# Second feed-forward product of a decoder layer: where GpSimd's sums, their loads and the side work stand in the order, and the first loads of a seam

## The chip, the cores and the metric

One core of a Trainium2 chip runs the whole program in one launch. The metric is the time of an execution on the device, in microseconds (us). Before the change three executions took 2927.35, 2926.52 and 2920.95 us; the median is 2926.52.

The engines have these names in the profile: PE is TensorE (matrix products), ACT is ScalarE, DVE is VectorE, POOL is GpSimd, and SP is SyncE, which here only issues DMA transfers (SPq in the profile). Each engine works through its own instructions in the order of the program and waits at an instruction until the data and the buffer that it needs are there.

## The reference

One layer of a decoder: a feed-forward network (FFN), token mixing by two branches (a pooling branch and a state-space branch), and a second FFN, on 1024 prompt tokens and 64 sample tokens, in float32. Cut to what matters here:

```python
def swiglu(x, w_in, w_out):
    gu = x @ w_in
    g, u = gu[..., :D_FF], gu[..., D_FF:]
    return (jax.nn.silu(g) * u) @ w_out

def layer(x, pool_hist, out_pos0, conv_hist, h0, l):
    x = x + 0.5 * swiglu(rmsnorm(x, norm_ffn1[l]), ffn1_w_in[l], ffn1_w_out[l])
    mix, ... = token_mixing(rmsnorm(x, norm_mix[l]), ...)
    x = x + mix
    x = x + 0.5 * swiglu(rmsnorm(x, norm_ffn2[l]), ffn2_w_in[l], ffn2_w_out[l])
    return x, ...

# in token_mixing: d is the trailing-window mean minus the token, in four groups of channels
y = jnp.einsum('btgc,gcd->btgd', d, w_group).reshape(Bsz, T, POOL_WIDTH)
```

D_MODEL is 1024, D_FF is 2816. The change touches the products with `w_out` of both FFNs, and the loads of `d` for the product with `w_group`.

## The kernel before

**Numbers.** Each float32 operand is split in a high part and a rest (`hh` and `hr` or the two halves of `hp` for the hidden values, `wh` and `wl` for weights): ACT writes the high part (L769, L787), DVE the rest (L770, L788), and PE adds three products, high x high, rest x high and high x low. The 1088 tokens are held in two halves of 512 and 576 tokens; a "pair" of matmuls below is the same step for both halves.

**The second product.** `second()` computes hidden x `w_out` in seven products of half the size (Strassen's scheme in a form with shared sums), in the order "1256473". A product has four units m (128 output channels each), and a unit has 11 blocks of k, whose weights come in three chunks of 4, 4 and 3 blocks. So a unit is 11 x 3 matmuls for each half, 66 in all. Product "3" is done half by half at the end; the others do both halves in a unit.

- The left operands (X) are sums of hidden blocks that the first product left in DRAM (`hb`). `fetch_X` loads them (L762, tiles `hr` and `hp`) and `split_X` splits them. `AHEAD` says how many of the next product's blocks are fetched behind a unit.
- The right operands are weights or sums of weights. `raw` loads a chunk (L776); for "1", "2" and "4" that is all. For "5" POOL adds two loaded chunks (L805, tile `ws`, kept), for "6" it subtracts a third from the kept one (L809), for "7" it takes a new difference (L814). `fourth(m)`, called behind each unit of "4", turns the kept chunk into the weights of "3" (L821, with one load at L776 into a `ws` tile).
- `leave` takes a unit's result out of PSUM on DVE (L863). After a unit of "6" it reloads a part of x from DRAM (L882, tile `x`), to which POOL adds after "4" (L885). `old` loads parts of the residual x after units of "6" and "7" (L827, tile `xo`); the additions on POOL (L833) are put into the list `late_` and made when the next unit is at its last chunk.

**Side work.** While FFN1 runs, `part` splits weights of later products and stores both parts in DRAM (load L313, tile `pr`; ACT L317, tile `ph`; DVE L318; stores L320 and L321). It is a generator that `tick` steps whenever PE's planned time has reached its due time; `finish(side)` runs what is left of it at once. FFN2 has no side work.

**The seam.** The pooling branch reads `d` (high part `dh`, rest `dl`) from DRAM, for two halves h and eight blocks k, two blocks for each of the four groups of channels (L1416). Six blocks are loaded ahead, at the end of the projections, the others by `fetch_d` one group ahead.

**What sets the order.** Python's order is only a start. A scheduler orders the instructions of each engine by its own estimate of times and by priorities (`tc.high_priority`), within the dependences; `pin` (that is, `tc.keep_in_program_order`) keeps an instruction in source order among those of its engine that are pinned too. Before the change pinned are, in this part, ACT's splits of X (L769), the side work's (L317) and POOL's sums L805 and L809, but not L814, L821, L833 and L885, nor the loads.

The buffers that bound how far a load can run ahead: six tiles for raw weights (`wraw`), three each for `wh` and `wl`, four `ws` tiles for the loads of "7" and of `fourth`.

Of the kernel before, what the change touches and what calls it, by code (L numbers as in the profile page):

```python
# [65 lines left out]
def tile_hybrid_pool_ssd_macaron(  # L66
# [588 lines left out]
    def ffn(wi, wo, prep, after, half, side=None):  # L655

        def plain(x):
            for ff in range(N_PLAIN[x[0]]):  # L660
                ffn_in_plain(wi, ff, x)

        X = operands(prep, plain)
        if side:
            side = start(side, PART_AT)
        for ff in range(N_PLAIN[1], N_PLAIN[0]):
            ffn_in(wi, ff, [(1, X[1])])
        for ff in range(N_PLAIN[0], NFF - N_APART):
            ffn_in(wi, ff, [(h, X[h]) for h in HALVES])
        front, run = second(wo, after, half)  # L670
        for h in HALVES:
            for ff in range(NFF - N_APART, NFF):
                if (h, ff) == (0, NFF - 1):
                    f = start(front(), X_FRONT)
                ffn_in(wi, ff, [(h, X[h])])
        if side:
            finish(side)
        finish(f)
        run()
# [62 lines left out]
    def second(wo, after, half):  # L742
# [29 lines left out]
        def raw(par, mh, m, kb, nk, t=None):  # L772
            if t is None:
                t = sp.tile([P, 4 * P], F32, tag="wraw", bufs=N_RAW, name=nm("wraw"))[:, : nk * P]
            c0 = (mh * 4 + m) * P
            dma(t.rearrange("p (k c) -> p k c", c=P), wv[par][:, kb : kb + nk, c0 : c0 + P])  # L776
            return t
# [13 lines left out]
        def weights(p, m):  # L791
            for kb, nk in chunks:
# [17 lines left out]
                else:  # L810
                    a = stage["p"].tile([P, 4 * P], F32, tag="wsum", bufs=N_S, name=nm("ws"))[:, : nk * P]
                    x, y = raw(0, 0, m, kb, nk, a), raw(0, 1, m, kb, nk)
                    with tc.high_priority(hp[0]):
                        G.tensor_tensor(a, x, y, op=ALU.subtract)  # L814
                yield (kb, nk) + parts(a, nk, ring("wh", nk), ring("wl", nk))

        def fourth(m):
            for kb, nk in chunks:
                t = stage["p"].tile([P, 4 * P], F32, tag="wsum", bufs=N_S, name=nm("ws"))[:, : nk * P]
                a, x = held[m, kb], raw(1, 0, m, kb, nk, t)  # L820
                G.tensor_tensor(a, x, a, op=ALU.subtract)  # L821

        def old(m, q, col):
            t = act((P, 576), name="xo")
            for h in HALVES:
                n, at = NPAIR[h], HALF_AT[h]
                dma(t[:, at : at + n], xspill[h][4 * q + m][:, col * n : (col + 1) * n])  # L827

            def put():
                for h in HALVES:  # L830
                    n, at = NPAIR[h], HALF_AT[h]
                    o = xt[h][4 * q + m][:, col * n : (col + 1) * n]
                    G.tensor_tensor(o, o, t[:, at : at + n], op=ALU.add)  # L833
# [24 lines left out]
        def leave(p, m, h, pt):  # L858
# [24 lines left out]
            elif p == "4":  # L883
                add(b[:, f], b[:, f])
                G.tensor_tensor(b[:, s_], b[:, s_], a[:, s_], op=ALU.add)  # L885
# [13 lines left out]
        def run():  # L899
            fetch_X("1", NK2)  # L900
            split_X(4)
            for p, nxt in zip(order[:-1], order[1:]):
# [3 lines left out]
                for m in range(4):  # L906
# [6 lines left out]
                    if p == "4":  # L913
                        fourth(m)
                    while p == "1" and hlast:
# [452 lines left out]
    def in_proj(prep):  # L1368
# [32 lines left out]
        ahead_d = []  # L1401
        for k in range(6):
            ahead_d.append(load_d(0, k))
# [57 lines left out]
    def pool_branch():  # L1461

        f = [([None] * KD, [None] * KD) for h in HALVES]
        d = dict(enumerate(ahead_d)), {}
# [553 lines left out]
```

## Time and profile before

| | us |
|---|---|
| executions (median 2926.52) | 2927.35, 2926.52, 2920.95 |
| profiled execution | 2930.37 |
| its span on the core | 2928.4 |
| mean granted clock of PE | 0.98 |
| second product of FFN1 | 529.11 to 794.06 |
| second product of FFN2 | 2656.97 to 2912.00 |
| seam into the pooling branch | about 1515 to 1560 |

The prediction quotes the views. A row of a timeline has the start and the duration in us, the engine, the line, the operation, its output and inputs, and how many instructions were merged; in brackets stands the idle time just before and what ended it. A row of the windows has the stretch, its length, the busy time of PE, PE's weight loads, DVE, ACT and POOL, the granted clock, the share of the DMA engines and GB/s. A row of the waits has who waited for whom: us in total, how often, the longest. Starts lie on one axis, from the span's start.

### The profile page before, as it was taken

Reading aid. Unit: us, or ns where it says so; the run is one execution under the profiler, and the core shown is the slowest. Engines: PE = TensorE matmul, PEld = TensorE weight load, DVE = VectorE, ACT = ScalarE, POOL = GpSimd, SP = SyncE. Lnnn points to the kernel's source line nnn. Section 1 sums busy time; section 2 is a strip of 40 time slices with the busy share of each in tenths; the row PEclk is TensorE's granted clock in tenths of the full one; section 3 lists DMA queues with packets and bytes.
Section 4 is the critical chain, followed back from the end, with each engine's and each line's share of the span. In section 5 each row is a group of like instructions: output and inputs, shape, how many; then the busy total and the mean of one; then the engine's idle time right before and its main releaser. Section 6 shows DMA issues by size and latency. Waiting matters only on the chain. (4 is left out here: it accounts for less than half of the span.)

```text
span 2928.4 us, 54549 instructions
## 1 busy us (share of the span) xinstructions
PE 2796.4 (95%) x19834; PEld 2617.3 (89%) x19834; DVE 1848.0 (63%) x2848; ACT 1399.7 (48%) x3086; POOL 1365.1 (47%) x1424
## 2 busy tenths in 40 slices
PE   7999999998999999999989999898999999999988
PEld 6999999898889999999988887677999999999987
DVE  6656556675784586866766767766666454556855
ACT  5444444433444555554546567576234444444333
POOL 5466566154542355554622333323225666561642
PEclk9999999999999999999999999998999999999999
DMA  4466545777445455543376567785674342336773
GB/s 123 146 195 213 160 151 173 222 220 236 149 124 166 149 181 173 188 132 122 106 238 201 184 232 231 246 254 185 228 252 145 112 125 88 99 122 208 225 226 107
DMA packets 567437, 515.25 MB, mean 176 GB/s; under 512 B 37876, under 2 KB 436072, under 8 KB 567160
## 3 DMA queue, kind: packets, MB, share of 16 engines
q1 hardware_dynamic: 564848, 507.31, 55.1%
q10 hardware_dynamic: 2320, 4.46, 0.4%
q8 instruction: 156, 2.56, 0.4%
q14 instruction: 113, 0.93, 0.1%
HBM read 363.51 MB, written 148.36 MB: 175 GB/s over the span
## 5 line engine op out<-in xcount | busy, mean ns | idle before, releaser
L167 PE MATMUL pw<-X,wh 128*128 128x288 f32 (+2 forms) x2832 | 627.2, 310 | 4.5 <-ACT v L569 4.5
L167 PEld LDWEIGHTS pw<-X,wh 128*128 128x128 f32 x2832 | 462.2, 189 | 26.9 <-ACT v L569 5.4
L167 PE MATMUL pw<-X,wl 128*128 128x288 f32 (+1 forms) x1644 | 473.9, 288 | 0.0
L167 PE MATMUL pw<-hl,wh 128*128 128x256 f32 (+1 forms) x1536 | 394.4, 329 | 0.6 <-ACT wh L452 0.4
L453 DVE TENSOR_TENSOR wl<-s,wh 128x512 fp32r<-128x512 f32 x288 | 231.7, 806 | 255.0 <-ACT wh L452 241.7
L446 POOL TENSOR_TENSOR s<-wraw,wraw 128x512 f32<-128x512 f32 x144 | 199.3, 1384 | 338.5 <-DVE wl L453 211.0
L167 PE MATMUL pw<-hi,wh 128*128 128x288 f32 x1120 | 330.8, 295 | 0.0
L167 PE MATMUL pw<-hi,wl 128*128 128x288 f32 x1120 | 329.8, 294 | 0.0
L167 PE MATMUL pw<-lo,wh 128*128 128x288 f32 x1120 | 329.7, 294 | 0.0
L167 PEld LDWEIGHTS pw<-X,wl 128*128 128x128 f32 x1644 | 312.0, 190 | 0.1
L167 PE MATMUL pw<-hl,wl 128*128 128x256 f32 x1072 | 301.4, 281 | 1.2 <-DVE wl L453 1.2
L167 PEld LDWEIGHTS pw<-hl,wh 128*128 128x128 f32 x1536 | 260.0, 190 | 22.1 <-ACT wh L452 0.6
L452 ACT ACTIVATE wh<-s 128x512 fp32r<-128x512 f32 x288 | 180.9, 630 | 163.4 <-PE pw L167 140.1
L453 DVE TENSOR_TENSOR wl<-wraw,wh 128x512 fp32r<-128x512 f32 x216 | 172.6, 799 | 135.2 <-ACT wh L452 126.7
L452 ACT ACTIVATE wh<-wraw 128x512 fp32r<-128x512 f32 x216 | 135.6, 628 | 174.1 <-PE pw L167 151.4
L167 PEld LDWEIGHTS pw<-hi,wh 128*128 128x128 f32 x1120 | 210.7, 188 | 6.4
L167 PEld LDWEIGHTS pw<-lo,wh 128*128 128x128 f32 x1120 | 210.7, 188 | 0.0
L167 PEld LDWEIGHTS pw<-hi,wl 128*128 128x128 f32 x1120 | 210.2, 188 | 0.0
L167 PEld LDWEIGHTS pw<-hl,wl 128*128 128x128 f32 x1072 | 204.1, 190 | 1.4 <-DVE wl L453 1.4
L167 PE MATMUL po<-hh,wh 128*128 128x256 f32 (+1 forms) x848 | 185.9, 290 | 5.8 <-ACT hh L769 5.8
L167 PE MATMUL po<-hr,wh 128*128 128x256 f32 (+1 forms) x848 | 186.9, 291 | 3.2 <-DVE hr L770 3.2
L167 PE MATMUL pso<-yhl,wh 128*128 128x288 f32 (+1 forms) x768 | 181.8, 339 | 4.8 <-ACT acc L1818 3.3
(400 smaller groups left out, 6844.9 us busy)
## 6 DMA issues: line engine op xcount, KB each, us to landing
wraw<-in_ffn_w_in_dram SPq DMA_DIRECT2D x188, 256.0 KB
wraw<-in_w_in_dram SPq DMA_DIRECT2D x144, 256.0 KB
wh<-part SPq DMA_DIRECT2D x116, 256.0 KB
wl<-part SPq DMA_DIRECT2D x116, 256.0 KB
hr<-hb SPq DMA_DIRECT2D x106, 272.0 KB
wraw<-in_ffn_w_out_dram SPq DMA_DIRECT2D x96, 256.0 KB
hb<-g SPq DMA_DIRECT2D x66, 288.0 KB
hb<-g SPq DMA_DIRECT2D x66, 256.0 KB
```

The costliest lines, as they stand in the source:

```text
L167: T.matmul(out, lhsT, rhs, start=start, stop=stop, skip_group_check=free)
L446: G.tensor_tensor(t, a, b, op=op)
L452: S.activation(wh, a, AF.Copy)
L453: V.tensor_tensor(wl, a, wh.bitcast(F32), op=ALU.subtract)
```

## The change

Three parts:

1. `ffn` no longer finishes the side work before the second product. It hands `side` to `run`, which finishes it behind the first unit of product "2".
2. In `second`, the loads of `fourth` are pinned, and so are POOL's differences for "7" (L814) and "3" (L821), the additions of the old x (L833) with their loads (L827), and the addition in `leave` after "4" (L885).
3. Of the six blocks of `d` that are loaded ahead, two are now of the second half: (0,0), (0,1), (1,0), (1,1), (0,2), (0,3) in place of the first half's 0 to 5.

```diff
@@ -673,10 +673,8 @@
                 if (h, ff) == (0, NFF - 1):
                     f = start(front(), X_FRONT)
                 ffn_in(wi, ff, [(h, X[h])])
-        if side:
-            finish(side)
         finish(f)
-        run()
+        run(side)
 
     def rest(c, gen):
         finish(c)
@@ -769,11 +767,13 @@
                 pin(S.activation(a, r, AF.Copy))
                 V.tensor_tensor(r.bitcast(F32R), r, a.bitcast(F32), op=ALU.subtract)
 
-        def raw(par, mh, m, kb, nk, t=None):
+        def raw(par, mh, m, kb, nk, t=None, fixed=False):
             if t is None:
                 t = sp.tile([P, 4 * P], F32, tag="wraw", bufs=N_RAW, name=nm("wraw"))[:, : nk * P]
             c0 = (mh * 4 + m) * P
-            dma(t.rearrange("p (k c) -> p k c", c=P), wv[par][:, kb : kb + nk, c0 : c0 + P])
+            ld = dma(t.rearrange("p (k c) -> p k c", c=P), wv[par][:, kb : kb + nk, c0 : c0 + P])
+            if fixed:
+                pin(ld)
             return t
 
         def ring(tag, nk):
@@ -811,26 +811,26 @@
                     a = stage["p"].tile([P, 4 * P], F32, tag="wsum", bufs=N_S, name=nm("ws"))[:, : nk * P]
                     x, y = raw(0, 0, m, kb, nk, a), raw(0, 1, m, kb, nk)
                     with tc.high_priority(hp[0]):
-                        G.tensor_tensor(a, x, y, op=ALU.subtract)
+                        pin(G.tensor_tensor(a, x, y, op=ALU.subtract))
                 yield (kb, nk) + parts(a, nk, ring("wh", nk), ring("wl", nk))
 
         def fourth(m):
             for kb, nk in chunks:
                 t = stage["p"].tile([P, 4 * P], F32, tag="wsum", bufs=N_S, name=nm("ws"))[:, : nk * P]
-                a, x = held[m, kb], raw(1, 0, m, kb, nk, t)
-                G.tensor_tensor(a, x, a, op=ALU.subtract)
+                a, x = held[m, kb], raw(1, 0, m, kb, nk, t, True)
+                pin(G.tensor_tensor(a, x, a, op=ALU.subtract))
 
         def old(m, q, col):
             t = act((P, 576), name="xo")
             for h in HALVES:
                 n, at = NPAIR[h], HALF_AT[h]
-                dma(t[:, at : at + n], xspill[h][4 * q + m][:, col * n : (col + 1) * n])
+                pin(dma(t[:, at : at + n], xspill[h][4 * q + m][:, col * n : (col + 1) * n]))
 
             def put():
                 for h in HALVES:
                     n, at = NPAIR[h], HALF_AT[h]
                     o = xt[h][4 * q + m][:, col * n : (col + 1) * n]
-                    G.tensor_tensor(o, o, t[:, at : at + n], op=ALU.add)
+                    pin(G.tensor_tensor(o, o, t[:, at : at + n], op=ALU.add))
 
             late_.append(put)
 
@@ -882,7 +882,7 @@
                 dma(b[:, s_], xspill[h][4 + m][:, s_])
             elif p == "4":
                 add(b[:, f], b[:, f])
-                G.tensor_tensor(b[:, s_], b[:, s_], a[:, s_], op=ALU.add)
+                pin(G.tensor_tensor(b[:, s_], b[:, s_], a[:, s_], op=ALU.add))
             elif p == "7":
                 add(b[:, f], b[:, f])
                 add(b[:, s_], b[:, s_])
@@ -896,7 +896,7 @@
                 split_X(k + 1)
                 yield 1.0
 
-        def run():
+        def run(side):
             fetch_X("1", NK2)
             split_X(4)
             for p, nxt in zip(order[:-1], order[1:]):
@@ -912,6 +912,8 @@
                         old(m, 0, 1)
                     if p == "4":
                         fourth(m)
+                    if side and p == "2" and m == 0:
+                        finish(side)
                     while p == "1" and hlast:
                         hlast.pop(0)()
                     while p == "1" and m == 2 and hsums:
@@ -1398,9 +1400,9 @@
             for kind, ia, ib in (("c", 16 + g, 20 + g), ("c", 4 * g, 4 * g + 1), ("c", 4 * g + 2, 4 * g + 3),
                                  ("u", 2 * g, 2 * g + 1), ("z", 4 * g, 4 * g + 1), ("z", 4 * g + 2, 4 * g + 3)):
                 proj_pair(kind, ia, ib, both)
-        ahead_d = []
-        for k in range(6):
-            ahead_d.append(load_d(0, k))
+        ahead_d = [{}, {}]
+        for h, k in ((0, 0), (0, 1), (1, 0), (1, 1), (0, 2), (0, 3)):
+            ahead_d[h][k] = load_d(h, k)
         for i in range(N_GATE[1], N_GATE[0], 2):
             proj_pair("g", i, i + 1, both[1:])
         last[0] = True
@@ -1461,7 +1463,7 @@
     def pool_branch():
 
         f = [([None] * KD, [None] * KD) for h in HALVES]
-        d = dict(enumerate(ahead_d)), {}
+        d = ahead_d
 
         def fetch_d(gi):
             for h in HALVES:
```

What this does to the order, at three places. In the names a number tells tiles apart; the lines are those of each kernel, so L762, L769 and L776 of before are L760, L767 and L774 in the changed one.

**ACT at the start of FFN1's second product.** `wh<-wraw` are weights of unit 0 of "1", `hh<-hr` blocks of X, `ph<-pr` side work, `g` is the end of the first product. Before:

```order
L787 ACTIVATE wh_6352<-wraw_6350 128x512
L787 ACTIVATE wh_6382<-wraw_6380 128x512
L610 ACTIVATE g_6166<-g_6166 128x288
L769 ACTIVATE hh_6168<-hr_6169 128x544
L769 ACTIVATE hh_6171<-hr_6172 128x544
L317 ACTIVATE ph_6310<-pr_6208 128x512
L787 ACTIVATE wh_6414<-wraw_6412 128x384
L317 ACTIVATE ph_6319<-pr_6317 128x512
L769 ACTIVATE hh_6174<-hr_6175 128x544
L769 ACTIVATE hh_6177<-hr_6178 128x544
L769 ACTIVATE hh_6180<-hr_6181 128x544
```

After the change:

```order
L787 ACTIVATE wh_6336<-wraw_6334 128x512
L317 ACTIVATE ph_6358<-pr_6208 128x512
L787 ACTIVATE wh_6373<-wraw_6371 128x512
L767 ACTIVATE hh_6320<-hr_6321 128x544
L610 ACTIVATE g_6166<-g_6166 128x288
L767 ACTIVATE hh_6168<-hr_6169 128x544
L767 ACTIVATE hh_6171<-hr_6172 128x544
L767 ACTIVATE hh_6174<-hr_6175 128x544
L767 ACTIVATE hh_6177<-hr_6178 128x544
L767 ACTIVATE hh_6180<-hr_6181 128x544
L767 ACTIVATE hh_6183<-hr_6184 128x544
```

The second of the two side splits, of `pr_6317`, is gone from here (the changed kernel has it as `pr_6403`, behind the second unit's X); one more block of X, `hr_6321`, stands early, and the third chunk of weights behind the blocks of X.

**SP from product "6" into "4" of FFN1** (FFN2 has the same). `xo` are the old x, `x<-xspill` the reload of `leave`, `ws` loads for the fourth sums, `wraw_8080` and up weights of "4", `hr` blocks of X for "4". Before:

```order
L827 DMA xo_7730<-xspill_0_83 128x256
L827 DMA xo_7730<-xspill_0_91 128x288
L827 DMA xo_7842<-xspill_1_84 128x256
L827 DMA xo_7842<-xspill_1_92 128x288
L762 DMA hr_7848<-hb_4_285 128x544
L762 DMA hr_7851<-hb_5_289 128x544
L776 DMA wraw_8080<-in_ffn_w_out_dram 128x4x128
L776 DMA wraw_8110<-in_ffn_w_out_dram 128x4x128
L776 DMA wraw_8140<-in_ffn_w_out_dram 128x3x128
L776 DMA wraw_8193<-in_ffn_w_out_dram 128x4x128
L776 DMA wraw_8223<-in_ffn_w_out_dram 128x4x128
L882 DMA x_7283<-xspill_4_87 128x256
```

After the change:

```order
L882 DMA x_7283<-xspill_4_87 128x256
L882 DMA x_7285<-xspill_4_95 128x288
L827 DMA xo_7730<-xspill_0_83 128x256
L827 DMA xo_7730<-xspill_0_91 128x288
L774 DMA wraw_8080<-in_ffn_w_out_dram 128x4x128
L774 DMA wraw_8110<-in_ffn_w_out_dram 128x4x128
L774 DMA wraw_8140<-in_ffn_w_out_dram 128x3x128
L774 DMA ws_8176<-in_ffn_w_out_dram 128x4x128
L774 DMA ws_8179<-in_ffn_w_out_dram 128x4x128
L882 DMA x_7394<-xspill_5_88 128x256
L774 DMA ws_8182<-in_ffn_w_out_dram 128x3x128
L882 DMA x_7396<-xspill_5_96 128x288
```

The reload of unit 0 (`x_7283`, `x_7285`) now precedes the old x of its unit, and the old x of unit 1 (`xo_7842`) goes behind the weights, the first fourth loads and the reload of unit 1. Before, eight more `ws` loads stood in one block behind `x_7285`; now they stand apart, the later ones behind the last X of "4".

**POOL in product "7" of FFN1** (FFN2 likewise). L814 of `ws_8769`, `ws_8802` and `ws_8835` are the weights of the third unit, of `ws_8890` and up those of the fourth. Before:

```order
L833 TENSOR_TENSOR x_6863<-x_6863,xo_8635 128x256
L833 TENSOR_TENSOR x_6865<-x_6865,xo_8635 128x288
L833 TENSOR_TENSOR x_6965<-x_6965,xo_8756 128x256
L833 TENSOR_TENSOR x_6967<-x_6967,xo_8756 128x288
L833 TENSOR_TENSOR x_7283<-x_7283,xo_8632 128x256
L814 TENSOR_TENSOR ws_8769<-ws_8769,wraw_8771 128x512
L833 TENSOR_TENSOR x_7285<-x_7285,xo_8632 128x288
L814 TENSOR_TENSOR ws_8802<-ws_8802,wraw_8804 128x512
L814 TENSOR_TENSOR ws_8835<-ws_8835,wraw_8837 128x384
L814 TENSOR_TENSOR ws_8890<-ws_8890,wraw_8892 128x512
L814 TENSOR_TENSOR ws_8923<-ws_8923,wraw_8925 128x512
```

After the change:

```order
L833 TENSOR_TENSOR x_7283<-x_7283,xo_8632 128x256
L833 TENSOR_TENSOR x_7285<-x_7285,xo_8632 128x288
L833 TENSOR_TENSOR x_6863<-x_6863,xo_8635 128x256
L833 TENSOR_TENSOR x_6865<-x_6865,xo_8635 128x288
L814 TENSOR_TENSOR ws_8769<-ws_8769,wraw_8771 128x512
L814 TENSOR_TENSOR ws_8802<-ws_8802,wraw_8804 128x512
L814 TENSOR_TENSOR ws_8835<-ws_8835,wraw_8837 128x384
L833 TENSOR_TENSOR x_7394<-x_7394,xo_8753 128x256
L833 TENSOR_TENSOR x_7396<-x_7396,xo_8753 128x288
L833 TENSOR_TENSOR x_6965<-x_6965,xo_8756 128x256
L833 TENSOR_TENSOR x_6967<-x_6967,xo_8756 128x288
L814 TENSOR_TENSOR ws_8890<-ws_8890,wraw_8892 128x512
```

The additions (L833) of a unit now stand together and ahead of the sums of the unit after the next: four instead of five before `ws_8769`, and four more before `ws_8890`.

## The prediction, made before the changed kernel was run

> **What bounds the kernel now.** I read the busy shares first, then the two stretches that hold the second product of each feed-forward network (FFN), then PE's waits. TensorE (PE) sets the end: it is busy 95% of the span, so a change pays only where PE stands still or runs slow.
>
> ```profile
> PE 2796.4 (95%) x19834; PEld 2617.3 (89%) x19834; DVE 1848.0 (63%) x2848; ACT 1399.7 (48%) x3086; POOL 1365.1 (47%) x1424
> ...
> 529.11:794.06 264.95, 243.80 (x1865) 240.82 (x1865) 177.71 (x250) 105.36 (x189) 113.96 (x97) 0.95 0.71 212
> 2656.97:2912.00 255.03, 238.84 (x1847) 234.69 (x1847) 161.16 (x231) 96.09 (x184) 102.76 (x86) 0.97 0.63 190
> ...
> PE po L167 <- ACT wh L787: 22.1, 6, 7.5
> PE pgm L167 <- DMA d<-dh: 7.6, 1, 7.6
> PE po L167 <- DVE wl L788: 6.9, 6, 1.9
> PE po L167 <- ACT hh L769: 5.8, 2, 5.4
> ```
>
> The second and third rows are the second products of FFN1 and FFN2: start:end, length, PE busy. One unit is 11 blocks of k by 3 terms by 2 halves, so 33 pairs of matmuls. Where nothing holds PE a pair starts every 0.25 us (543.00 and 543.25 below): 8.25 us a unit, 231 us for 28 units. So about 34 us are lost in FFN1 and 24 in FFN2. The last four rows name the waits, and PE's timeline the places:
>
> ```profile
> 537.46 0.82 PE L167 MATMUL po<-hh,wh 128*128 128x256 f32 x2 [5.42 <-ACT hh L769]
> ...
> 541.62 0.66 PE L167 MATMUL po<-hh,wl 128*128 128x256 f32 x2
> 542.07 0.59 PE L167 MATMUL po<-hh,wh 128*128 128x256 f32 x2
> ...
> 543.00 0.41 PE L167 MATMUL po<-hh,wh 128*128 128x256 f32 x2
> 543.25 0.41 PE L167 MATMUL po<-hr,wh 128*128 128x256 f32 x2
> ...
> 680.84 1.27 PE L167 MATMUL po<-hp,wh 128*128 128x256 f32 x4 [7.51 <-ACT wh L787]
> 683.97 0.82 PE L167 MATMUL po<-hp,wl 128*128 128x256 f32 x2 [1.85 <-DVE wl L788]
> ...
> 694.24 0.67 PE L167 MATMUL po<-hp,wh 128*128 128x256 f32 x4
> ...
> 739.28 0.76 PE L167 MATMUL po<-hp,wh 128*128 128x256 f32 x4 [3.08 <-ACT wh L787]
> 740.84 0.82 PE L167 MATMUL po<-hp,wl 128*128 128x256 f32 x2 [0.80 <-DVE wl L788]
> ...
> 744.04 0.66 PE L167 MATMUL po<-hp,wh 128*128 128x256 f32 x4
> ```
>
> A stall costs more than its length. Until 542.07 pairs start 0.45 us apart (541.62 to 542.07), from 543.00 on 0.25: PE runs at about half rate for some 5 us after a stop. The first unit of product "4" should start at 673.33 (680.84 - 7.51) and the next one starts at 694.24: 20.91 us for 8.25 of work, 12.7 lost for 9.36 of waiting, 1.35 times. At 739.28: 3.88 of waiting plus half rate until 744.04 (4.76 - 0.80 = 3.96 us, of which 0.20/0.45 is lost, 1.8): 5.6, 1.45 times. I price stalls at 1.4 times. The Trainium skill, "TensorE: Matmul & The Clock Gate", Part 1, states that the clock halves after about 3.4 us without work. By that rule the 3.08-us stop would have kept full rate; the row shows half rate, so the measurement decides here. By the rule, the stops of 1 and 2 us that I leave in part B would cost nothing beyond themselves, 8.6 in place of 10, and the sum would be 2.8 us better; no row shows a stop of that length by itself.
>
> **A, start of FFN1's second product.** The side work is no longer drained before the product starts: its last load goes behind the loads of X on SP, its last split among the units on ACT.
>
> ```profile
> 530.14 0.38 SPq L313 DMA_DIRECT2D pr<-in_w_o_dram  x1
> ...
> 537.99 1.88 SPq L762 DMA_DIRECT2D hr<-hb  x4
> ...
> 536.24 0.63 ACT L317 ACTIVATE ph<-pr 128x512 fp32r<-128x512 f32 x1 [5.70 <-DMA pr<-in_w_o_dram]
> ...
> 537.50 5.03 DVE L770 TENSOR_TENSOR hr<-hr,hh 128x544 fp32r<-128x544 f32 x5
> 543.60 2.61 DVE L770 TENSOR_TENSOR hr<-hr,hh 128x544 fp32r<-128x544 f32 x3
> ```
>
> ScalarE (ACT) waits 5.70 us for pr, the blocks of X queue behind it, and the loads of k 7 to 10 leave SP at 537.99 only. This costs 5.42, plus 4.61 us at half rate (537.46 to 542.07), 2.05 of it lost: 7.5. Afterwards neither stands in front. What is late next is VectorE (DVE): eleven X blocks at 0.87 to 1.01 (2.61/3, 5.03/5) and two weight splits of about 1.1 are 11.8 to 13.3 us against PE's 8.25; the earliest block and one weight split lie ahead of PE's start, so 2 to 5 us stay, I take 3. **Gain 4.5**, bounds 2 (pr and the four loads now crowd the queue ahead of the weights) and 7. The moved split (one ACT, one DVE instruction, two stores, one load) falls into units where both engines have idle time; without that cover it costs 0.63 + 0.69. FFN2 has no side work: nothing there.
>
> **B, product "6" into "4", both FFNs.** The fourth sums' loads used to be hoisted ahead of their units; now they follow them. But the old x loads (L827) are now pinned behind leave's reloads (L882).
>
> ```profile
> 641.64 2.85 SPq L827 DMA_DIRECT2D xo<-xspill  x4
> ...
> 661.18 0.81 SPq L882 DMA_DIRECT2D x<-xspill  x2
> ...
> 662.52 10.52 SPq L776 DMA_DIRECT2D ws<-in_ffn_w_out_dram  x8
> ...
> 675.10 0.84 SPq L762 DMA_DIRECT2D hr<-hb  x2
> ...
> 678.83 1.44 ACT L769 ACTIVATE hh<-hr 128x544 fp32r<-128x544 f32 x2 [13.38 <-DMA hr<-hb]
> ...
> 647.47 0.74 POOL L833 TENSOR_TENSOR x<-x,xo 128x256 f32<-128x256 f32 x1 [2.35 <-DMA xo<-xspill]
> ...
> 650.21 4.81 POOL L809 TENSOR_TENSOR ws<-ws,wraw 128x512 f32<-128x512 f32 x3
> ...
> 664.10 2.03 POOL L885 TENSOR_TENSOR x<-x,x 128x256 f32<-128x256 f32 x2 [2.43 <-DMA x<-xspill]
> ...
> 649.53 0.45 DVE L863 SCALAR_TENSOR_TENSOR x<-po,t 128x288 f32<-128x288 f32 x1
> ```
>
> Removed: eight ws loads hold SP for 10.52 us, since each needs a fourth sum to free its tile; hr of "4" waits behind them, ACT behind hr, and the weights behind ACT. That is the 12.7. Added: in "6" GpSimd (POOL) makes the additions of unit m-2 ahead of the sums of unit m, and xo now leaves SP only after leave, which ended at 649.98 for unit 0 (649.53 + 0.45). Two x issues take 0.8, so xo leaves at 650.8 and lands 2.9 later (661.18 to 664.10) at 653.7; two additions of 0.8 and one sum of 1.6 (4.81/3) bring 656.9, ACT and DVE some 1.3 more. PE wants unit 2 at 656.67 (673.33 - 2 x 8.25): about 1 us late. For unit 3 xo stands also behind a weight load whose place is freed by unit 2's last sum (655.3 + 4.8 = 660.1): seven issues of 0.42 bring 663.0, landing 665.9, additions and sum 669.1, split 670 against 665.9 wanted: 4 late. The last hr of "4" stand behind the reload of unit 3, whose leave follows PE's end: about 2 late by the same steps. 7 us by 1.4 is 10. **Gain 12.7 - 10 = 2.5 for each FFN.** Bounds: landing of 5.8 as on the busier queue (641.64 to 647.47) makes about 15 of stalls, 21 lost, 8 worse; where xo comes in time at all three places the 10 go too. I stay with 2.9, since the row is from just this reload. The twelve fourth sums now run under "4", on a POOL that is busy for 113.96 of this stretch's 264.95 us; their readers come two products later, so they cost nothing. Without that cover each would cost about a sum's 1.6.
>
> **C, product "7", third unit, both FFNs.**
>
> ```profile
> 723.08 0.37 SPq L776 DMA_DIRECT2D wraw<-in_ffn_w_out_dram  x1
> 723.50 3.83 SPq L827 DMA_DIRECT2D xo<-xspill  x8
> ...
> 729.65 5.18 POOL L833 TENSOR_TENSOR x<-x,xo 128x256 f32<-128x256 f32 x5 [5.06 <-DMA xo<-xspill]
> 734.79 1.29 POOL L814 TENSOR_TENSOR ws<-ws,wraw 128x512 f32<-128x512 f32 x1
> ...
> 736.11 0.63 ACT L787 ACTIVATE wh<-ws 128x512 fp32r<-128x512 f32 x1 [6.26 <-POOL ws L814]
> ```
>
> POOL waits 5.06 for xo and makes five additions before the sum that the third unit needs; on ACT, splits for product "3" stand ahead of that unit's. Afterwards the two weight loads that held SP until 723.08 come behind the sums' loads, four additions precede the sum, and "3" comes after. The first addition now needs leave of unit 0, which ends with the unit at 736.2 - 8.25 = 727.95, so 728.9 for the first half; four of 1.0 (5.18/5) bring 732.9, sum 734.2, splits 735.5, wanted at 736.2. It fits by 0.7 us; unit 3 likewise. **Gain 5 of the 5.6, each**; bounds 2 (the sum late by a landing) and 5.6.
>
> **D, the seam into the pooling branch.**
>
> ```profile
> 1521.81 0.51 SPq L1416 DMA_DIRECT2D d<-dh  x1
> ...
> 1528.29 2.13 PE L167 MATMUL pgm<-d,wh 128*128 128x288 f32 x5 [7.60 <-DMA d<-dh]
> ...
> 1532.69 0.63 PE L167 MATMUL pgm<-d,wh 128*128 128x512 f32 x2
> ```
>
> The stall of 7.60 waits for the second half's first d, issued 6.5 us earlier. Those now come ahead; but the second half's k 2 and 3 take their place in the queue, and the bytes are the same. The second half's first groups took 4.4 us at half rate (1528.29 to 1532.69), some 2.2 at full; with the first half's next groups, at 0.7 each (1532.69), PE gets about 4 us of work to do inside the old stall, then waits again. **Gain 4**, bounds 0 (it only moves) and 8 (no half rate after it).
>
> **Sum.** 4.5 + 2 x 2.5 + 2 x 5 + 4 = 23.5. The profiled execution took 2930.4 (span 2928.4), so about 2907; it lies 3.9 above the median of the runs, 2926.5, and I take half of that off: **2905**. Bounds of the terms together, by the profiled execution: from a loss of 10 (2 - 16 + 4 + 0) to a gain of 51 (7 + 2 x 12.5 + 11 + 8).
>
> **Rivals.** (1) Slower, about 2938: xo under leave. If landing takes the 5.8 of the busy queue, POOL's source order makes every second unit of "6" wait: 8 worse for each FFN; "7" then gains 2 each, A and D may be down to 2 and 0: 16 - 6 = +10. It decides from a landing of about 5 us. For it: the DMA share of 0.71 in the quoted row; against: the 2.9 of the reload. (2) Load-bound, about 2916: A and B and D only shift waits, since the same bytes arrive at the same rate; C's 10 and 2 of A remain, 2930 - 12. For it: a stall of d that its own issue times explain. Against: A's 5.70 is a load issued late, not slowly. (3) All stalls go, about 2878: the upper bounds together. For it: DVE and POOL are idle by a third or more in these stretches; against: the xo chain worked out above. (4) The pins change nothing on the path, since the tile waits stay: 2926; against: the order of instructions does change at each of the places.
>
> **Numbers.** Forecast 0.46, rival 1 0.17, rival 2 0.20, rival 3 0.12, rival 4 0.05. A measurement here tells 0.2%, about 6 us, from no change. Faster takes all of the forecast and rival 3 and most of rival 2: 0.71; same 0.13 (rival 4, parts of 1 and 2); slower 0.16. The range of 8 in 10 reaches from 2884, where part of rival 3 is left out, to 2928, where most of rival 1 is; the forecast's own is 2893 to 2915.
>
> **What would show it.** A: ACT's wait on pr gone, X loads k 7 to 10 issued before 530, PE's first two units near 20 us. B: no 10-us block of ws loads on SP; PE waits of about 1 and 4 us at units 2 and 3 of "6" instead of 7.5 at "4". C: no PE wait over 1 us in "7". D: the wait on d at half its length, later. I would be wrong if POOL's wait for xo in "6" exceeds 5 us, or if the d wait only changes place.

## The result, and the profile after

The changed kernel takes 2927.16 us (median of 12 executions, 2921.89 to 2929.39), the kernel before 2926.86 in the same series (12 executions). The ratio is 1.000, with a 95% interval of 0.999 to 1.001: no difference, where a gain of 21 us was forecast. The profiled execution of the changed kernel took 2925.94 us.

The page of the changed kernel, its busy times and PE's longest waits (who waited for whom: us in total, how often, the longest):

```profile
PE 2798.1 (96%) x19834; PEld 2614.3 (89%) x19834; DVE 1857.1 (64%) x2848; ACT 1400.7 (48%) x3086; POOL 1370.1 (47%) x1424
...
PE po L167 <- ACT wh L787: 15.5, 7, 3.8
PE po L167 <- DVE hr L768: 10.2, 20, 1.9
PE po L167 <- ACT hh L767: 6.3, 5, 2.9
PE po L167 <- DVE wl L788: 6.1, 11, 0.9
...
PE pgm L167 <- DMA d<-dh: 1.2, 1, 1.2
```

PE's own 2798 us hold the half rate behind its stops too, so the gain has to be looked for in the waits. The 7.6 us for d are down to 1.2, and the waits for high parts of weights fell from 22.1 to 15.5. But PE waits 38.1 us in all for the second products' operands (15.5 + 10.2 + 6.3 + 6.1) where it waited 38.0 before (22.1 + 6.9 + 5.8, and 3.2 for `hr`). The stops were not removed; they were cut into more, smaller ones.

Where they are shows when the second product of FFN1 is cut at its products. A product ends here where PE has done its last matmul, so a stop between two products counts for the second one. These are the windows of products 6, 4 and 7, first of the kernel before, then of the changed one (start:end, length, busy time of PE, PE's weight loads, DVE, ACT, POOL, granted clock, DMA share, GB/s):

```profile
640.17:673.33 33.16, 33.16 (x266) 32.94 (x264) 25.49 (x33) 10.84 (x19) 26.70 (x22) 1.00 0.66 191
673.33:719.32 45.99, 36.63 (x266) 36.31 (x266) 27.56 (x38) 16.20 (x29) 18.54 (x18) 0.85 0.86 260
719.32:758.29 38.97, 35.09 (x266) 34.65 (x265) 25.40 (x36) 14.65 (x27) 24.61 (x22) 0.96 0.68 200
```

```profile
636.19:675.73 39.54, 35.79 (x267) 35.39 (x265) 20.44 (x36) 11.97 (x21) 11.60 (x12) 0.91 0.61 179
675.73:716.48 40.75, 35.47 (x267) 34.55 (x265) 32.22 (x35) 14.53 (x25) 31.98 (x25) 0.96 0.73 217
716.48:757.31 40.83, 35.88 (x266) 34.73 (x265) 30.00 (x38) 15.41 (x28) 26.16 (x23) 0.96 0.89 253
```

A product needs 33 us of PE (four units of 8.25). Product 6 became 6.4 us longer. Product 4 became 5.2 us shorter: its stop of 7.51 us at the start is gone, but three smaller ones came; more of POOL's fourth sums lie there too (31.98 us of POOL instead of 18.54). Product 7 became 1.9 us longer. The lead of 4.0 us with which the changed kernel enters product 6 (640.17 - 636.19), which is about part A's gain, is down to 1.0 at the end of 7. PE's timeline of the changed kernel has the stops behind this:

```profile
664.93 1.28 PE L167 MATMUL po<-hp,wh 128*128 128x256 f32 x4 [3.75 <-ACT wh L787]
...
685.12 0.52 PE L167 MATMUL po<-hh,wh 128*128 128x256 f32 x2 [2.86 <-ACT hh L767]
...
689.62 0.52 PE L167 MATMUL po<-hr,wh 128*128 128x256 f32 x2 [1.89 <-DVE hr L768]
...
691.09 0.82 PE L167 MATMUL po<-hr,wh 128*128 128x256 f32 x2 [0.45 <-DVE hr L768]
...
737.44 0.77 PE L167 MATMUL po<-hp,wh 128*128 128x256 f32 x4 [3.33 <-ACT wh L787]
```

3.75 is the start of unit 3 of product 6; 2.86, 1.89 and 0.45 are late blocks of X in product 4; 3.33 is the third unit of product 7, as before (3.08).

### The profile page after: what moved, and what is told of

Same layout as the page of the kernel before. It is cut to its first block, busy times and chain, and to the rows that moved or that the text cites. A ratio compares the mean times of both kernels' runs of the same rounds, so it can differ in the third digit from the quotient of the medians.

```text
span 2924.2 us, 54556 instructions
## 1 busy us (share of the span) xinstructions
PE 2798.1 (96%) x19834; PEld 2614.3 (89%) x19834; DVE 1857.1 (64%) x2848; ACT 1400.7 (48%) x3086; POOL 1370.1 (47%) x1424
## 5 line engine op out<-in xcount | busy, mean ns | idle before, releaser
L167 PE MATMUL po<-hr,wh 128*128 128x256 f32 (+1 forms) x848 | 188.2, 293 | 10.3 <-DVE hr L768 10.2
L167 PE MATMUL po<-hh,wl 128*128 128x256 f32 (+1 forms) x848 | 186.0, 290 | 0.5 <-DVE wl L788 0.3
```

The costliest lines, as they stand in the source:

```text
L167: T.matmul(out, lhsT, rhs, start=start, stop=stop, skip_group_check=free)
```

## The experiments

e1 to e8 are the kernel before with some of the edits of the diff; e9 to e14 have an edit more. Times are medians, ratios are against the kernel before on the same chip, in brackets their 95% interval. The rows come from several chips, so differences in us below are worked out from the ratios where nothing else is said; each is uncertain by 3 to 4 us.

| kernel | what it has | us | ratio |
|---|---|---|---|
| the changed kernel | all | 2927.2 | 1.000 [0.999, 1.001] |
| e1 | A: the side work | 2922.3 | 0.9984 [0.9972, 0.9995] |
| e2 | D: the loads of d | 2919.7 | 0.9975 [0.9963, 0.9987] |
| e3 | A and D | 2917.2 | 0.9969 [0.9959, 0.9980] |
| e4 | all the pins | 2937.6 | 1.0038 [1.0024, 1.0051] |
| e5 | A, D, pins on L827 and L833 | 2920.2 | 0.9973 [0.9962, 0.9984] |
| e6 | A, D, pins on the fourth loads, L821, L885 | 2914.1 | 0.9955 [0.9943, 0.9968] |
| e7 | the changed kernel, L827 not pinned | 2914.8 | 0.9959 [0.9946, 0.9971] |
| e8 | A, D, pin on L833 | 2917.0 | 0.9968 [0.9956, 0.9980] |
| e9 | e7, old x of product 7 after its last unit | 2916.3 | 0.9966 [0.9954, 0.9979] |
| e10 | e7, old x of product 7 one unit later | 2917.4 | 0.9964 [0.9952, 0.9976] |
| e11 | the changed kernel, old x as in e9 | 2931.1 | 1.0016 [1.0005, 1.0026] |
| e12 | e7 and paired loads in product 7 | 2894.5 | 0.9887 [0.9874, 0.9900] |
| e13 | A, D, pin on L814, paired loads | 2928.0 | 1.0002 [0.9994, 1.0011] |
| e14 | the changed kernel and paired loads | 2924.2 | 0.9992 [0.9981, 1.0003] |

And the lengths of the products in the profiled executions, cut as above, FFN1 / FFN2, in us. The last column runs from where DVE begins to take the last unit of 7 out of PSUM (L863) to where it begins to take the fourth unit of 3. Each of these executions lies within 5 us of its kernel's median.

| kernel | 6 | 4 | 7 | 3, four first-half units |
|---|---|---|---|---|
| before | 33.2 / 33.3 | 46.0 / 44.7 | 39.0 / 38.9 | 16.8 / 22.2 |
| changed | 39.5 / 40.2 | 40.8 / 39.8 | 40.8 / 41.0 | 18.0 / 23.4 |
| e3 | 33.2 / 33.2 | 46.9 / 45.3 | 38.9 / 40.8 | 16.8 / 22.2 |
| e4 | 39.5 / 39.7 | 40.7 / 38.2 | 41.5 / 43.9 | 18.1 / 23.4 |
| e5 | 42.8 / 42.5 | 38.5 / 38.4 | 36.6 / 37.2 | 18.0 / 23.4 |
| e6 | 33.2 / 33.0 | 33.2 / 35.6 | 50.5 / 49.8 | 16.8 / 22.2 |
| e7 | 33.0 / 33.0 | 35.4 / 34.5 | 43.9 / 48.7 | 18.0 / 23.4 |
| e8 | 33.2 / 33.2 | 45.3 / 44.9 | 38.6 / 37.7 | 18.0 / 23.4 |
| e9 | 33.0 / 33.0 | 35.4 / 33.4 | 44.0 / 48.3 | 23.2 / 25.0 |
| e10 | 33.0 / 33.0 | 33.2 / 33.4 | 49.9 / 47.3 | 20.0 / 23.5 |
| e11 | 39.3 / 40.2 | 41.2 / 41.2 | 38.5 / 39.0 | 23.7 / 23.2 |
| e12 | 33.0 / 33.0 | 33.2 / 33.2 | 39.5 / 38.9 | 18.0 / 22.9 |
| e13 | 33.2 / 33.2 | 45.1 / 45.8 | 45.8 / 44.7 | 16.9 / 21.1 |
| e14 | 39.3 / 40.7 | 40.2 / 38.5 | 40.6 / 40.4 | 18.0 / 22.9 |

### Is the zero a sum?

Theory 1: gains and losses that cancel. Theory 2: each part is hidden by something that sets the end anyway. The first kernel has part A alone:

```diff
-        if side:
-            finish(side)
         finish(f)
-        run()
+        run(side)
...
+                    if side and p == "2" and m == 0:
+                        finish(side)
```

> Only the later draining of the side work (part A), everything else as before. Theory 1 (the change is a sum of gains and losses that cancel: A gives 4, the seam 5 to 6, the pins take back 4 in FFN1 and 5 in FFN2): about 4 us faster than before, 0.9986; the end of FFN1's second product 4 us earlier against its start, ACT's 5.4 us wait gone. Theory 2 (each part is hidden by something later that sets the end anyway): no difference, the lead of A is gone by the end of product 3 of FFN1 without any pin.

The second has the loads of d alone:

```diff
-        for k in range(6):
-            ahead_d.append(load_d(0, k))
+        for h, k in ((0, 0), (0, 1), (1, 0), (1, 1), (0, 2), (0, 3)):
+            ahead_d[h][k] = load_d(h, k)
```

> Only the other order of the first loads of d (part D). Theory 1: about 5.5 us faster, 0.998; the 7.6 us wait on d becomes one or two of about 1 us, and the stretch from the first pgm matmul to 1600 is 5 to 6 us shorter. Theory 2: no difference; the waits on d only move to later groups.

The third has both, and the fourth only the pins (the rest of the diff).

> A and D together, no pins. Theory 1: 9 to 10 us faster than before, 0.9967, and so faster than the changed kernel as well. Theory 2: within 2 us of before.

> Only the pins in the second product (parts B and C), for both FFNs, no A and no D. Theory 1: 9 to 10 us slower than before, 1.0033: in each FFN the stall of 7.5 at the start of product 4 is replaced by one of 3.8 in unit 3 of product 6, one of 2 to 3 in unit 0 of product 4 and one of 1 to 2 in its unit 1, and the 3-us stall in product 7 stays. Theory 2 (the changed kernel is the same as before in each part): no difference.

Measured: 0.9984 for A (4.7 us), 0.9975 for D (7.3 us), 0.9969 for both (9.1 us), 1.0038 for the pins (11.1 us lost). 4.7 + 7.3 - 11.1 is 0.9, and 9.1 - 11.1 is -2.0; both agree with no difference within the intervals. Theory 1 holds, and theory 2 is out, since each part alone differs from the kernel before. The pins lose what the table of products shows: product 7 grows by 2.5 and 5.0 us, product 3 by 1.2 in each FFN, products 6 and 4 together by 1.1 and by nothing: 11.0 us in all.

### Which pin loses?

Theory P: the pinned old x loads (L827). Theory Q: the fourth loads, which now crowd products 4 and 7. The first kernel pins only the old x loads and their additions, the second only the fourth loads, their sums and leave's addition:

```diff
-                dma(t[:, at : at + n], xspill[h][4 * q + m][:, col * n : (col + 1) * n])
+                pin(dma(t[:, at : at + n], xspill[h][4 * q + m][:, col * n : (col + 1) * n]))
...
-                    G.tensor_tensor(o, o, t[:, at : at + n], op=ALU.add)
+                    pin(G.tensor_tensor(o, o, t[:, at : at + n], op=ALU.add))
```

> A and D as in the faster combination, plus only two of the pins: the old x loads (L827) and their additions (L833). The fourth loads stay free. Theory P (the pinned old x loads, now behind leave's reload and behind the weights of product 4, make the late sums in unit 3 of product 6 and the late X in product 4): slower than A and D together by 8 us or more, about 2926 or above, with the 3.8-us stall in unit 3 of product 6 in both FFNs. Theory Q (the fourth loads, moved behind their units, crowd SP in products 4 and 7): within 2 us of A and D together, 2917.

```diff
-                a, x = held[m, kb], raw(1, 0, m, kb, nk, t)
-                G.tensor_tensor(a, x, a, op=ALU.subtract)
+                a, x = held[m, kb], raw(1, 0, m, kb, nk, t, True)
+                pin(G.tensor_tensor(a, x, a, op=ALU.subtract))
...
-                G.tensor_tensor(b[:, s_], b[:, s_], a[:, s_], op=ALU.add)
+                pin(G.tensor_tensor(b[:, s_], b[:, s_], a[:, s_], op=ALU.add))
```

> A and D plus only the pins of the fourth loads, the fourth sums (L821) and leave's additions (L885); old x free. Theory P: the block of ws loads at the start of product 4 is gone and nothing takes its place: the 7.5-us stall falls below 3, so 10 us or more faster than A and D together, about 2905. Theory Q: the loads that left product 6 hold SP in products 4 and 7; what is won at the start of 4 is lost there, within 3 us of 2917, with more waiting in product 7 than the 3.9 us of before.

The third is the changed kernel with one pin less, the fourth has only the pin on POOL's additions:

```diff
-                pin(dma(t[:, at : at + n], xspill[h][4 * q + m][:, col * n : (col + 1) * n]))
+                dma(t[:, at : at + n], xspill[h][4 * q + m][:, col * n : (col + 1) * n])
```

> The changed kernel with one pin taken away, that of the old x loads (L827); POOL's order is exactly that of the changed kernel. Theory P: the stall in unit 3 of product 6 goes, as in the run with the fourth pins alone, and the time is that run's, 15 us or more below the changed kernel. Theory Q: no faster than the changed kernel by more than 3 us, about 2924 to 2927. A third reading, that POOL's order of additions is at fault and not the loads: the stall of unit 3 of product 6 stays at 3 to 4 us.

> A and D plus only the pins of the old x additions on POOL (L833), loads free: SP's order is that of A and D, POOL's changes in products 6 and 7. Theory P and Q: within 2 us of A and D together. The third reading (POOL's order): slower by 4 us or more. If the additions in product 7 are what its third unit waits for, its 3-us stall gets shorter here by 1 us or more, since four additions precede the sum instead of five.

Both theories hold a part, and both were too simple. The fourth pins take away the stop at the start of product 4: against e3, e6 gains 13.7 and 9.7 us in product 4, and product 6 stays at PE's own time. Theory Q is right about the giving back: e6 loses 11.7 and 8.9 us of this in product 7. Taking the pin off the old x loads makes the changed kernel 12 us faster (2927.2 to 2914.8), although POOL's order stays the same: so the loads, not the additions, cost it. e8 agrees: with only the additions pinned it has the ratio of e3, although product 3 pays 1.2 us for them. But the old x pins without the fourth pins (e5) cost only 1 us against e3 (3 by the medians, on different chips), which the intervals do not tell from nothing, and not the 8 that theory P expected. There the stops of product 6 (1.5 and 4.5 us at units 2 and 3) stand in place of the stop at the start of product 4, which the hoisted fourth loads make anyway: products 6 and 4 of FFN1 take 81.4 us together in e5 and 80.0 in e3. So what a pin costs depends on the others, and the costs cannot be added pin by pin.

The chain of the changed kernel at unit 3 of product 6, on SP, POOL and ACT:

```profile
651.33 3.04 SPq L774 DMA_DIRECT2D wraw<-in_ffn_w_out_dram  x3
...
657.12 0.83 SPq L827 DMA_DIRECT2D xo<-xspill  x2
...
680.50 1.38 SPq L760 DMA_DIRECT2D hr<-hb  x3
...
661.52 1.47 POOL L833 TENSOR_TENSOR x<-x,xo 128x256 f32<-128x256 f32 x2 [7.55 <-DMA xo<-xspill]
...
664.25 0.63 ACT L787 ACTIVATE wh<-ws 128x512 fp32r<-128x512 f32 x1 [9.17 <-POOL ws L809]
...
684.41 0.66 ACT L767 ACTIVATE hh<-hr 128x544 fp32r<-128x544 f32 x1 [5.10 <-DMA hr<-hb]
```

The three weight loads of product 4 leave SP between 651.33 and 654.37, each when a sum of unit 2 has freed its place; xo leaves at 657.12, behind them and behind the fourth loads and the reloads of unit 1 that follow them, and is there at 661.52; POOL had nothing to do for 7.55 us, because its next sum stands behind that addition; ACT splits at 664.25 and PE goes on at 664.93. And the last X of product 4 stand behind the reload of unit 3 (680.50) and stop PE at 685.12. With the old x loads free (e7) the loads of this row had left by 638, and none of these stops exists.

### Why did part C gain nothing?

The first idea was that in product 7 the loads of the sums stand behind eight old x loads on SP (reading 1), against a general lateness (reading 2). So the old x of product 7 went behind its last unit, in e7 and in the changed kernel, or one unit later:

```diff
-                    elif p == "7":
-                        old(m, 1, 0)
-                        old(m, 0, 1)
+                    elif p == "7" and m == 3:
+                        for q in range(4):
+                            old(q, 1, 0)
+                            old(q, 0, 1)
```

> The changed kernel without the pin on the old x loads (the run at 0.9959), and the old x of product 7 loaded and added only behind its last unit instead of behind each. Reading 1 (in product 7 the sums of the third unit are late because their loads stand behind eight old x loads on SP): the stalls of 6.0 and 7.5 us at unit 2 of product 7 fall below 2, about 16 us less in both FFNs, so about 2899; product 3 may give back a few, since sixteen additions come there at once. Reading 2 (they are late because the fourth loads put SP and the DMA engines behind, whatever order follows): the stall stays above 4, the time within 4 us of 2915.

> As the run before, but the old x of product 7 only one unit later than now (units 2 and 3 together at the end). Reading 1: the stall at unit 2 falls to about half, since four old x loads instead of eight are ahead of its sums, about 8 us less than 2915 in all. Reading 2: within 4 us of 2915.

> The changed kernel with all its pins, and only the old x of product 7 behind its last unit. Reading 1: the 3.3 and 2.6 us stalls at unit 2 of product 7 go, 4 to 5 us each with the half rate after them: 8 to 10 us faster than the changed kernel, about 2918. Reading 2: within 3 us of the changed kernel. The stalls in products 6 and 4 stay in both.

Reading 1 falls. Product 7 keeps 44.0 and 48.3 us in e9 (43.9 and 48.7 before the edit). The stop at the start of unit 2 did go, but one as long now stands within unit 1, 7.36 us in FFN1 and 6.99 in FFN2:

```profile
722.98 0.82 PE L167 MATMUL po<-hh,wh 128*128 128x256 f32 x2 [7.36 <-ACT wh L787]
```

Product 3 pays 5.2 and 1.6 us for the sixteen additions. e10 has stops of 6.32 and 5.29 us in the same unit. e11 gains nothing on the changed kernel either: by the ratios it is about 5 us slower, at the edge of what the intervals tell. The times of e9 and e10 are those of reading 2, but that names no load. The rows of the changed kernel suggested another reading: a sum of product 7 needs two loads, `ws` and `wraw`, and the scheduler lets the `wraw` run ahead.

```profile
712.77 4.48 SPq L774 DMA_DIRECT2D wraw<-in_ffn_w_out_dram  x4
...
719.79 0.38 SPq L774 DMA_DIRECT2D ws<-in_ffn_w_out_dram  x1
...
722.06 1.02 SPq L774 DMA_DIRECT2D wraw<-in_ffn_w_out_dram  x2
723.46 6.31 SPq L827 DMA_DIRECT2D xo<-xspill  x8
...
731.11 1.48 SPq L774 DMA_DIRECT2D ws<-in_ffn_w_out_dram  x3
...
725.98 1.28 POOL L814 TENSOR_TENSOR ws<-ws,wraw 128x512 f32<-128x512 f32 x1 [6.01 <-DMA ws<-in_ffn_w_out_dram]
...
730.29 4.23 POOL L833 TENSOR_TENSOR x<-x,xo 128x256 f32<-128x256 f32 x4 [1.80 <-DMA xo<-xspill]
735.46 3.90 POOL L814 TENSOR_TENSOR ws<-ws,wraw 128x512 f32<-128x512 f32 x3 [0.94 <-DMA ws<-in_ffn_w_out_dram]
```

SP spends 4.48 us on four `wraw`, the last of them for unit 2, and some X loads follow, before it gets to the `ws` of unit 1 at 719.79, for which POOL waits 6.01 us; the `ws` of unit 2 leave at 731.11, and their first sum, at 735.46, is what PE waits for until 737.44. So both loads of each sum were pinned in source order (reading 3), against the reading that four `ws` places bound product 7 in any order (reading 4):

```diff
-                    x, y = raw(0, 0, m, kb, nk, a), raw(0, 1, m, kb, nk)
+                    x, y = raw(0, 0, m, kb, nk, a, True), raw(0, 1, m, kb, nk, fixed=True)
```

> The changed kernel without the pin on the old x loads, and the two loads of each sum of product 7 pinned in source order, so that they leave SP pair by pair (ws, wraw, ws, wraw) and no raw load of unit 3 stands ahead of unit 2's pairs. Reading 3 (unit 2 waits because SP stands at a raw load of unit 3, whose place is freed only by a sum of unit 1, with unit 2's own loads behind it): the stalls of 6.0 and 7.5 at unit 2 go, 8 to 10 us each with the half rate: 2900 or less. Reading 4 (four ws places and the two loads that each chunk needs bound product 7 in any order): the waits of product 7 together stay above 5 us in each FFN, the time within 4 us of 2915.

> A and D and the paired loads and pinned sums of product 7, no other pin, so that the fourth loads run during product 6 as before. Reading 3: the 2.4 and 3.8 us stalls at unit 2 go, 4 to 5 us each: about 8 us below A and D together (2917), about 2908, while the 8 us stall at the start of product 4 stays. Reading 4: within 3 us of 2917, since the stalls of product 7 are only moved to other units.

> The changed kernel with all its pins and the paired loads of product 7. Reading 3: the 3.3 and 2.6 us stalls at unit 2 go: 7 to 10 us faster than the changed kernel, about 2918, and the stalls of products 6 and 4 stay. Reading 4: within 3 us of the changed kernel.

In e7 and e12, which differ in nothing else, the stop at unit 2 in FFN1 is 5.97 us and none. First e7, SP, POOL and PE:

```profile
707.64 0.38 SPq L774 DMA_DIRECT2D ws<-in_ffn_w_out_dram  x1
713.12 0.37 SPq L774 DMA_DIRECT2D wraw<-in_ffn_w_out_dram  x1
...
718.66 1.48 SPq L774 DMA_DIRECT2D ws<-in_ffn_w_out_dram  x3
...
711.81 1.29 POOL L814 TENSOR_TENSOR ws<-ws,wraw 128x512 f32<-128x512 f32 x1 [10.29 <-DMA ws<-in_ffn_w_out_dram]
...
723.78 3.45 POOL L814 TENSOR_TENSOR ws<-ws,wraw 128x512 f32<-128x512 f32 x3 [2.42 <-DMA ws<-in_ffn_w_out_dram]
...
726.27 1.28 PE L167 MATMUL po<-hp,wh 128*128 128x256 f32 x4 [5.97 <-ACT wh L787]
```

Between 708.02 and 713.12 SP stands at a `wraw` of the last unit, until a sum (711.81 to 713.10) frees its place; unit 2's three `ws` leave at 718.66. In e12, SP, POOL and the window of product 7:

```profile
712.62 0.38 SPq L774 DMA_DIRECT2D ws<-in_ffn_w_out_dram  x1
713.06 0.50 SPq L774 DMA_DIRECT2D wraw<-in_ffn_w_out_dram  x1
...
719.11 4.92 POOL L814 TENSOR_TENSOR ws<-ws,wraw 128x512 f32<-128x512 f32 x3
...
701.64:741.14 39.50, 35.23 (x264) 34.62 (x265) 29.71 (x38) 15.95 (x29) 30.14 (x24) 0.96 0.96 273
```

The pairs leave together, unit 2's first at 712.62, and its sums run without a wait. In FFN2 the stop at unit 2 falls from 7.52 to 1.09 us. Product 7 falls from 43.9 and 48.7 to 39.5 and 38.9, its stops together from 7.2 and 11.1 us to 4.3 in each FFN. Between these two kernels reading 3 holds: the stop that it named goes, and the time is 21 us lower, where reading 4 had at least 5 us of stops and about 2915 us. In the changed kernel (e14) the stop at unit 2 goes too, but stops of 1.97 and 2.62 us come back at the first unit, product 7 keeps 40.6 and 40.4 us, and the stops of 6 and 4 stay: 0.9992, which the intervals do not tell from the changed kernel. So reading 3 missed its 7 to 10 us there, and the time is the one that reading 4 gave. Pairing also moves some X loads behind the pairs; that was not tried apart.

The second of these runs missed both readings: e13 has the pairs without the pins of the fourth loads and of the additions, and is 10 us slower than e3. Here the stop at unit 2 is gone but one of 3.84 us stands at unit 3. On POOL and PE:

```profile
744.38 1.49 POOL L833 TENSOR_TENSOR x<-x,xo 128x256 f32<-128x256 f32 x2 [2.88 <-DVE x L863]
745.83 3.90 POOL L814 TENSOR_TENSOR ws<-ws,wraw 128x512 f32<-128x512 f32 x3
...
747.81 1.28 PE L167 MATMUL po<-hp,wh 128*128 128x256 f32 x4 [3.84 <-ACT wh L787]
```

Left free, an addition that needs unit 2's result got ahead of unit 3's sums on POOL: the sums could only start when PE had already run out of them. This suggests that the pin on the additions, which by itself gains nothing (e8), is what makes the paired loads pay. It is not shown apart, since e13 lacks the fourth pins as well.

e12 beats both kernels: 2894.5 us, 0.9887 of before. It is the changed kernel without the pin on the old x loads and with the two loads of each sum of product 7 pinned as well. Its gain on the kernel before lies in product 4 (46.0 and 44.7 us, now 33.2 in both); product 7 is about as long as it was. The fourth pins take the stop out of product 4, the free old x loads keep it out of product 6, and the pairs keep it out of product 7.

## Why the prediction was wrong, point by point

**A, the side work: right.** 4.5 was forecast, 4.7 measured alone, with an interval from 1.5 to 8.2. ACT's 5.7-us wait is gone, and the X loads of k 7 to 10 leave at 520.45, before 530 as forecast. The 3 us left for DVE are there too: 1.62 us of short waits in the first units and one spell of 3.41 us at half rate.

**D, the seam: right mechanism, perhaps too small.** 4 forecast, 7.3 measured, with an interval from 3.8 to 10.8. The wait moved and shrank as described; in the changed kernel PE and SP show:

```profile
1528.69 0.72 PE L167 MATMUL pgm<-d,wh 128*128 128x512 f32 x2 [1.74 <-DVE fl L364]
...
1531.50 0.50 PE L167 MATMUL pgm<-d,wh 128*128 128x288 f32 x2 [1.18 <-DMA d<-dh]
...
1526.01 0.32 SPq L1418 DMA_DIRECT2D d<-dh  x1
```

The second half's k 2 leaves SP at 1526.01, and PE has it 5.5 us later, as expected of a load that takes the place of the old one. The term that looks too small is the work that PE can do meanwhile: PE is busy from 1519.70 to 1526.95 and, behind the wait of 1.74, to 1530.3, not for 4 us.

**B, product 6 into 4: the first failed step.** "7 us by 1.4 is 10. Gain 12.7 - 10 = 2.5 for each FFN." With the pins alone, products 6 and 4 lose 1.1 us in FFN1 and gain nothing in FFN2; in the changed kernel they lose 1.1 and 2.1. The stop at the start of product 4 went as forecast. Of the three residual stops that the prediction worked out, unit 3's was right in size (4 forecast, 3.75 measured) and by the chain that it described, with some luck: xo left about 2 us earlier against PE than worked out and took 4.4 us to land in place of 2.9. Unit 2's of 1 did not come (old x was there within 2.3 us of its issue). The late X of product 4 were put at 2 and cost three stops, 2.86 + 1.89 + 0.45 = 5.2. And the multiplier failed. 8.95 us of stops cost 14.3 us in FFN1 (39.54 + 40.75 - 66), 1.6 times (1.8 in FFN2), where 9.36 us in two stops had cost 13.2 by the same cut, 1.4 times. The stretches at half clock show part of the reason, first before the change, then in the changed kernel:

```profile
675.57:689.23 13.66, 6.54 (x27) 6.22 (x28) 7.63 (x11) 4.08 (x7) 10.69 (x11) 0.50 0.74 227
...
663.27:670.10 6.83, 5.17 (x22) 5.01 (x23) 5.19 (x9) 2.77 (x5) 3.58 (x3) 0.50 0.40 109
690.58:693.99 3.41, 2.96 (x14) 2.90 (x14) 2.29 (x5) 2.04 (x4) 3.41 (x4) 0.50 0.87 271
```

Before, PE stood still anyway for more than half of its time at half clock and worked for 6.54 us of it. In the changed kernel it works for 5.17 + 2.96 = 8.13 us at half clock, behind shorter stops. The factor had been taken from places with one stop or two close together.

**C, product 7: the second failed step, and the larger one.** "It fits by 0.7 us ... Gain 5 of the 5.6, each." Measured: product 7 became 1.9 and 2.1 us longer, and 2.5 and 5.0 with the pins alone. The order on POOL was as described. The premise that old x would leave earlier, since two weight loads no longer stood in front, was wrong: two loads of unit 2's own sums (722.06) now stand there, and old x left at 723.46, before it was 723.50. So the additions began at 730.29 only, as soon as xo was there, and the `ws` of unit 2, which left behind old x at 731.11, held the sum until 735.46. SP was late from product 4 on, where the fourth loads now are; those were costed at nothing because their readers come late. That reader was the wrong one to look at: what the loads delay is whatever stands behind them on SP. e6, which pins them with their sums and leaves old x free, shows the price: 11.7 and 8.9 us in product 7.

**Sum and rivals.** A and D gave 9.1 us together where 8.5 were forecast, B and C lost 11.1 where 15 of gain were forecast. The sign that the prediction gave for being wrong came: POOL waits 7.55 us for xo in product 6, more than 5. Rival 1 named the place, old x behind leave, and gave it 0.17. But it was to decide only from a landing of 5 us; the landings were 2.3 and 4.4 us, and the pins on old x cost 12 us all the same, through the weight loads that it stands behind and the half rate of each stop. Rival 3, all stops gone at 2878, is reached by two thirds in e12, with another set of pins. Rival 4 (no effect, 2926) fits the total and not the reason; rival 2 (2916) fits neither, since the gain of C that it kept did not come.

The trace and the clock rule: the prediction weighed the Trainium skill, "TensorE: Matmul & The Clock Gate", Part 1, by which the clock halves after about 3.4 us without work, so that shorter stops would cost nothing beyond themselves. The trace agrees with the 3.4 us as the length of the steps in which the granted clock changes (3.41), and not with the condition: in the step ahead of one spell of half rate PE was busy for 2.17 us and had no stop above 0.66, as the last section shows.

## What to carry to other kernels

Pinning an instruction to source order pins it behind everything that was pinned before it, and on an in-order queue it then waits for their buffers too: look at what stands in front of each pinned load, not only at what stands behind. An operation that needs two loads wants both pinned together, or one runs ahead and holds the queue against the other half of an earlier pair. When stops are traded, count the stops as well as their sum, since each one can bring its own slow restart.

## What the hardware showed that was not expected

PE fell to half rate without any stop above 0.7 us. In the changed kernel at the start of FFN1's second product, after waits of 0.42, 0.66 and 0.16, PE's rows and then the windows around them:

```profile
527.34 0.52 PE L167 MATMUL po<-hh,wh 128*128 128x256 f32 x2 [0.42 <-ACT hh L767]
528.52 0.52 PE L167 MATMUL po<-hr,wh 128*128 128x256 f32 x2 [0.66 <-DVE hr L768]
...
529.70 0.52 PE L167 MATMUL po<-hr,wh 128*128 128x256 f32 x2 [0.16 <-DVE hr L768]
...
526.74:530.15 3.41, 2.17 (x13) 1.55 (x12) 3.41 (x5) 3.41 (x8) 3.33 (x3) 1.00 1.05 352
530.15:533.57 3.42, 3.42 (x16) 3.23 (x15) 3.42 (x5) 1.20 (x3) 1.33 (x2) 0.50 0.99 290
533.57:536.98 3.41, 3.39 (x28) 3.17 (x26) 3.41 (x5) 2.47 (x5) 3.12 (x3) 1.00 0.22 66
```

The granted clock is 0.50 from 530.15 to 533.57 and 1.00 on both sides. Every spell at 0.50 that is shown here lasts 3.41 us or a multiple of it (6.83 and 13.66 above), and in one trace they begin whole steps apart: from 530.15 to 663.27 are 39 steps of 3.413. In e12 a single stop of 1.54 us was followed by full rate:

```profile
733.28 0.52 PE L167 MATMUL po<-hp,wl 128*128 128x256 f32 x2 [1.54 <-DVE wl L788]
...
732.07:735.48 3.41, 2.19 (x17) 2.20 (x18) 3.41 (x6) 1.91 (x4) 3.41 (x4) 1.00 0.69 186
735.48:738.90 3.42, 3.42 (x30) 3.42 (x29) 3.01 (x3) 1.21 (x3) 1.83 (x2) 1.00 0.97 285
```

So the length of one stop does not decide by itself. Nor do these rows show that PE's busy time within one step does: it was 2.17 us in the step that half rate followed, and 2.19 us in the one of e12, cut on that trace's own steps, that it did not follow. What decides was not settled here.
